# A decoder layer: where one residual is scaled and shifted, where a row of sums of squares is made, and which form its reciprocal root has

## The chip, the cores and the metric

The kernel runs on one core of one Trainium2 chip. The metric is the time of one execution on the device in microseconds (us); the kernel before was run three times. The engines are TensorE (PE, with its weight loads as PEld), VectorE (DVE), ScalarE (ACT), GpSimd (POOL) and the queue engine SyncE (SP), which only issues transfers here. Each engine works through its own list of instructions in order.

## The reference

One layer over 1024 positions of width 1024 with 16 learned meta tokens in front, all in float32:

```python
h = layer_norm(concat([meta, x]), ln_emb_g, ln_emb_b)
proj = h @ w_in                       # q, k, v, xr, gr, 512 columns each
attn = stick_breaking(q, k, v)        # 8 heads of 64
lru = rg_lru(conv(xr), ...) * gelu(gr)
mixed = concat([rms_norm(attn, attn_norm_g), rms_norm(lru, lru_norm_g)]) @ w_out
h = layer_norm(ALPHA * h + mixed, ln1_g, ln1_b)          # ALPHA = 2 ** 0.25
h = layer_norm(ALPHA * h + peer(h), ln2_g, ln2_b)        # retrieval of 16 of 16384 experts per head
return h[:, 16:]
```

Two things in it matter here. The residual `ALPHA * h` of the first layer norm needs that norm's own scale and shift: with the normalised input n it is `n * (ALPHA * g) + ALPHA * b`. And each RMS norm is a factor per position, so it can be put on the product with `w_out` afterwards: 1 / sqrt(mean of squares + 1e-5), one number for each row.

## The kernel before, in words

Positions lie on the 128 partitions, eight tiles of them (j = 0 to 7), the width of 1024 along the free axis. A float32 product is made of three passes of split operands (`mm3`, L126: low x high, high x high, high x low), so each operand is split once: ACT rounds the high part, DVE subtracts it for the low part (`split`, L122; DVE's part is L124).

The stages that matter here, with their times in the profiled execution:

1. **Front** (0 to about 50 us). Nine input tiles `xt` are loaded. DVE makes their statistics, ACT normalises them in place (L281), and POOL issues eight transfers of the normalised tiles to a scratch tensor `xh_d` in device memory (L283). PE transposes the tiles in three groups (L287 to L292), ACT puts scale and shift on the transposed copy (L294), and the copy is split into `hT` (L297, L299, L300). PE begins the projections with it (`pieces`, L223) while later groups are still being made.
2. **Recurrent part** (to about 200 us): `lru_in` (DVE's convolution, `y`, L346 and L348), `lru_gates`, and the values of the attention (`values_w` splits the weights `v`, `values` multiplies). The pools `lr` and `l2` of this stage take the memory that the front's pools `ga` and `lw` give back.
3. **Attention**, four pairs of heads p, each over eight tiles j. `att_a` makes scores, two sigmoids, a running product (DVE scan `om`, L481) and a product (DVE `be`, L482) for each of two heads; `att_b` transposes the result, copies it out of the accumulators (L505, L507) and multiplies it with the values (`po`, L513). While p is 0 to 2, projections for the next pair are put between. At p = 2, j = 6, the projection's memory is given back and the output weights are loaded and split (`load_wo`, L445); also the scale and shift of the first layer norm (`eg`, `eb`), which ACT multiplies by ALPHA (L592, L593). At p = 3 the recurrent half of the out-projection goes between instead: `lru_load` (L552) brings a tile `hr` of `xh_d` back, POOL multiplies it by `eg` and adds `eb` (L556, L557), `lru_mix` (L560) adds the product to it on DVE (L567) and stores it to `ah_d`. `hr` and the raw output weights share one name (`raw`) with two buffers. `att_a` also has POOL copy two small operands (`qz`, L465).
4. **Out-projection** (`mix_out`, about 556 to 645 us). `prep(j)` (L626) loads the attention tile, squares it (`sq`, one buffer), splits it, and makes the sums of squares `ss` by four matmuls with a column of ones (L633) and the reciprocal root `rra` by `rsqrt_small` (L131: ACT root, DVE reciprocal, and one step of improvement in four DVE instructions of which three have two inputs from memory). `body(j)` (L638) runs the 24 matmuls of each tile in two halves of 512 columns, adds each half to the residual (L645) and takes the layer norm, whose own root is `rsqrt_one` (L143: the step of improvement in three DVE instructions, each with one input tensor and numbers per partition). `tail(j)` (L648) transposes and splits the result and has POOL scale and shift it (L651, L652). In program order `prep(j + 1)` stands ahead of `body(j)`.
5. The expert retrieval, to the end.

The order on each engine is not the program order. The library's scheduler plays the program through with estimated durations and issues on each engine, when it is free, the ready instruction that comes first in program order. Instructions that go through `W` or `pin` keep their place behind what stands ahead of them on their engine. Once planned, the order is fixed, and each engine waits at an instruction whose inputs are late.

## Time and profile before

| | |
|---|---|
| median of three runs | 2960.87 us (2960.4 to 2962.03) |
| profiled execution | 2963.82 us, span 2962.0 us |
| busy in the span | PE 2783.2, DVE 2487.0, POOL 1453.4, ACT 1148.1 us |
| mean granted TensorE clock | 0.973 |

The profile is of one execution. A busy share is a mean over stages with different limits, so each stage is read by itself: what its engines do, which of them waits for what, and which steps are on the chain that ends last. The granted clock is a share of full speed: 1.00 is 2.4 GHz and 0.50 is 1.2 GHz. A wait is put down to the instruction that released it.

### The profile page before, as it was taken

The numbers are of one execution on the slowest core, as the hardware profiler recorded it, in microseconds if no ns is written. First come the engines' busy times: TensorE is split into PE (matmuls) and PEld (weight loads), VectorE is DVE, ScalarE is ACT, GpSimd is POOL, SyncE is SP. The second block draws the span as 40 slices with busy tenths as digits, with TensorE's granted clock in tenths as the row PEclk, the third lists the DMA queues.
The fourth block names the chain that finished last, engine by engine and source line by source line (L and its number), as shares of the span: only waits on it lengthen the run. The fifth ranks groups of instructions, "written<-read, shape, count | busy, mean of one in ns | idle before, by whom it ended". The sixth has DMA issues, their size and how long they took to land.

```text
span 2962.0 us, 44399 instructions
## 1 busy us (share of the span) xinstructions
PE 2783.2 (94%) x16311; PEld 2492.6 (84%) x16311; DVE 2487.0 (84%) x4610; ACT 1148.1 (39%) x2245; POOL 1453.4 (49%) x1202
## 2 busy tenths in 40 slices
PE   7999988889879989899989999999999999999997
PEld 6997766679879988889888888888888888888886
DVE  6246667768999999998769999999999999899997
ACT  6445553452212239787752223222222232222222
POOL 0003223343676655645435555556555666665653
PEclk9999988899989999999999999999999999999999
DMA  5123143413656668888789999999999999999992
GB/s 175 30 79 72 39 99 125 149 52 109 218 182 231 229 222 275 276 272 265 236 286 343 353 351 345 347 357 350 335 356 359 349 340 353 350 346 352 334 325 79
DMA packets 353946, 736.32 MB, mean 249 GB/s; under 512 B 26032, under 2 KB 164272, under 8 KB 353728
## 3 DMA queue, kind: packets, MB, share of 16 engines
q0 software_dynamic: 114304, 415.35, 39.5%
q1 hardware_dynamic: 234816, 316.03, 31.7%
q8 instruction: 128, 2.10, 0.3%
q10 hardware_dynamic: 4608, 2.10, 0.2%
q14 instruction: 90, 0.74, 0.1%
HBM read 645.24 MB, written 79.69 MB: 245 GB/s over the span
## 4 chain that ended last, share of the span: by engine, by line
PE 34%; DVE 23%; issue 17%; POOL 12%; DMA 11%; ACT 3%; SPq 0%; POOLq 0%; DVEq 0%; ACTq 0%
POOL row L894 9%; DMA row<-up,idx 6%; DVE row L113 4%; PE pp L127 3%; PE dps L127 3%; PE pp L128 3%; PE dps L129 3%; PE dps L128 3%; PE pp L129 3%; DVE dl L124 2%; DMA row<-down,idx 2%; PE g L1026 2%; PE po L513 2%; DVE h1s L1082 2%; PE z L127 2%
## 5 line engine op out<-in xcount | busy, mean ns | idle before, releaser
L127 PE MATMUL dps<-hTd,dl 128*128 128x320 f32 x2048 | 651.2, 318 | 47.0 <-DVE dl L124 40.7
L129 PE MATMUL dps<-hTd,dh 128*128 128x320 f32 x2048 | 646.6, 316 | 2.0 <-DVE hTd L124 2.0
L128 PE MATMUL dps<-hTd,dh 128*128 128x320 f32 x2048 | 647.3, 316 | 0.0
L894 POOL DMA_INDIRECT row<-down,idx x256 | 357.6, 1397 | 226.5 <-DVE act L113 188.8
L894 POOL DMA_INDIRECT row<-up,idx x256 | 343.6, 1342 | 233.9 <-DVE h1s L1082 196.3
L127 PEld LDWEIGHTS dps<-hTd,dl 128*128 128x128 f32 x2048 | 391.2, 191 | 53.0 <-DVE dl L124 32.9
L127 PE MATMUL ups<-uh,wl 128*128 128x512 f32 x1024 | 406.9, 397 | 2.6 <-DVE wl L124 2.0
L128 PE MATMUL ups<-uh,wh 128*128 128x512 f32 x1024 | 406.9, 397 | 0.0
L129 PE MATMUL ups<-ul,wh 128*128 128x512 f32 x1024 | 406.2, 397 | 0.5 <-DVE ul L124 0.5
L128 PEld LDWEIGHTS dps<-hTd,dh 128*128 128x128 f32 x2048 | 391.5, 191 | 3.0
L129 PEld LDWEIGHTS dps<-hTd,dh 128*128 128x128 f32 x2048 | 390.7, 191 | 2.3 <-DVE hTd L124 2.3
L1082 DVE SCALAR_TENSOR_TENSOR h1s<-row,gws,h1s 128x1024 f32<-128x1024 f32 x256 | 328.2, 1282 | 29.6 <-DMA row<-up,idx 27.5
L113 DVE CUSTOM_DVE_ANT_0 row<-row,h1s 128x1024 f32<-128x1024 f32 x256 | 307.1, 1221 | 36.8 <-DMA row<-down,idx 34.3
L123 ACT ACTIVATE wh<-gl 128x640 fp32r<-128x640 f32 x128 | 101.3, 792 | 606.4 <-DVE gl L1138 344.6
L894 POOL DMA_INDIRECT row<-up,idh x128 | 185.4, 1448 | 233.3 <-DVE acc L1072 84.4
L124 DVE TENSOR_TENSOR dl<-raw,dh 128x1024 fp32r<-128x1024 f32 x144 | 192.5, 1338 | 64.3 <-ACT dh L123 57.7
L129 PEld LDWEIGHTS ups<-ul,wh 128*128 128x128 f32 x1024 | 193.3, 189 | 48.3 <-DVE ul L124 1.0
L127 PEld LDWEIGHTS ups<-uh,wl 128*128 128x128 f32 x1024 | 193.2, 189 | 47.6 <-DVE wl L124 2.4
L128 PEld LDWEIGHTS ups<-uh,wh 128*128 128x128 f32 x1024 | 193.1, 189 | 44.0
L894 POOL DMA_INDIRECT row<-down,idh x128 | 162.2, 1267 | 136.2 <-DVE ach L113 23.8
L123 ACT ACTIVATE uh<-raw 128x1024 fp32r<-128x1024 f32 x128 | 133.0, 1056 | 176.5 <-PE keep L128 167.0
L113 DVE CUSTOM_DVE_ANT_0 row<-row,acc 128x1024 f32<-128x1024 f32 x128 | 176.1, 1381 | 13.0 <-DMA row<-down,idh 13.0
(583 smaller groups left out, 6194.3 us busy)
## 6 DMA issues: line engine op xcount, KB each, us to landing
raw<-downT SPq DMA_DIRECT2D x128, 512.0 KB
raw<-up SPq DMA_DIRECT2D x128, 512.0 KB
Gd<-gst SPq DMA_DIRECT2D x20, 2048.0 KB
gl<-Gd SPq DMA_DIRECT2D x128, 320.0 KB
ge_d<-ge SPq DMA_DIRECT2D x56, 320.0 KB
gex<-ge_d SPq DMA_DIRECT2D x56, 320.0 KB
wraw<-w_in SPq DMA_DIRECT2D x20, 512.0 KB
raw<-wq SPq DMA_DIRECT2D x16, 512.0 KB
```

The lines of the kernel that those rows point to most:

```text
L113: return lambda *a, **k: pin(getattr(V, name)(*a, **k))
L123: A.activation(hi, src, AF.Copy)
L124: V.tensor_tensor(lo, src, hi.bitcast(F32), op=ALU.subtract)
L127: PE.matmul(o, ll, rh, start=start, stop=False, **kw)
L128: PE.matmul(o, lh, rh, start=False, stop=False, **kw)
L129: PE.matmul(o, lh, rl, start=False, stop=stop, **kw)
L513: PE.matmul(po[64 * e:64 * e + 64], vt[:m, b, p * P + 64 * e:p * P + 64 * e + 64], aTs[e][:m, b], start=(b == 0), stop=(b == nb - 1))
L894: G.indirect_dma_start(out=row, out_offset=None, in_=src, in_offset=bass.IndirectOffsetOnAxis(ap=ix, axis=0))
L1026: PE.matmul(gpt[:, q], bt[:, q], at[:, q], start=True, stop=True)
L1082: pin(V.scalar_tensor_tensor(h1s[:, j], row, gws[:, j, s:s + 1], h1s[:, j], op0=ALU.mult, op1=ALU.add))
```

## The change

The scale and shift of the residual move from POOL at p = 3 to DVE at the front: `eg` and `eb` are loaded and multiplied by ALPHA there, in the pool `ga`, and after the three groups DVE multiplies and adds each of the eight tiles `xt` in place; SP instead of POOL then stores them to `xh_d`. At p = 3 the tile from `xh_d` is used as it comes. In `mix_out`, the sums of squares of a tile and their root move from `prep(j)` to `body(j)`, between the two halves of its matmuls; both halves are added to the residual after the second one, and the root has the form of `rsqrt_one`, whose two small tiles it now shares with the layer norm.

```diff
@@ front @@
                 for j in range(j0, j1):
                     n = NM if j == 0 else P
                     A.activation(xts[j][:n], xts[j][:n], AF.Identity, bias=nm9[:n, j:j + 1], scale=rs9[:n, j:j + 1])
-                    if j > 0:
-                        G.dma_start(xh_d[(j - 1) * P:j * P, :], xts[j])
...
                 for xr, gen in convs.values():
                     next(gen)
+            eg = load_vec(ga, 0, "eg")
+            eb = load_vec(ga, 1, "eb")
+            A.activation(eg, eg, AF.Copy, scale=ALPHA)
+            A.activation(eb, eb, AF.Copy, scale=ALPHA)
+            for j in range(1, NT + 1):
+                V.tensor_tensor(xts[j], xts[j], eg, op=ALU.mult)
+                V.tensor_tensor(xts[j], xts[j], eb, op=ALU.add)
+                SY.dma_start(xh_d[(j - 1) * P:j * P, :], xts[j])
@@ lru_load @@
                 SY.dma_start(hr, xh_d[j * P:(j + 1) * P, :])
-                G.tensor_tensor(hr, hr, eg, op=ALU.mult)
-                G.tensor_tensor(hr, hr, eb, op=ALU.add)
@@ attention, p == 2 and j == 6 @@
-                        eg = load_vec(mp, 0, "eg")
-                        eb = load_vec(mp, 1, "eb")
-                        A.activation(eg, eg, AF.Copy, scale=ALPHA)
-                        A.activation(eb, eb, AF.Copy, scale=ALPHA)
@@ mix_out @@
             def prep(j):
                 mh, ml, sq = first if j == 0 else mixed(0, j)
                 SY.dma_start(h1[j], ah_d[j * P:(j + 1) * P, :])
-                mv = wm.tile([P, 1], F32, name="mva")
-                rra = wm.tile([P, 1], F32, name="rra")
-                ss = sps.tile([P, 1], F32, name="ss")
-                for c in range(4):
-                    PE.matmul(ss, sq[:, c], ones, start=(c == 0), stop=(c == 3))
-                V.tensor_scalar(mv, ss, 1.0 / AW, EPS, op0=ALU.mult, op1=ALU.add)
-                rsqrt_small(rra, mv, P, 1, "ra", wm)
-                return mh, ml, rra
-
-            def body(j, mh, ml, rra):
+                return mh, ml, sq
+
+            def body(j, mh, ml, sq):
+                halves = []
                 for hf in range(2):
...
                         mm3(ps, mh[:, c], ml[:, c], wh[:, cs], wl[:, cs], c == 0, c == 3)
+                    halves.append((cs, ps))
+                    if hf == 0:
+                        mv = wm.tile([P, 1], F32, name="mva")
+                        rra = wm.tile([P, 1], F32, name="rra")
+                        ss = sps.tile([P, 1], F32, name="ss")
+                        for c in range(4):
+                            PE.matmul(ss, sq[:, c], ones, start=(c == 0), stop=(c == 3))
+                        V.tensor_scalar(mv, ss, 1.0 / AW, EPS, op0=ALU.mult, op1=ALU.add)
+                        rsqrt_one(rra, mv, P)
+                for cs, ps in halves:
                     V.scalar_tensor_tensor(h1[j][:, cs], ps, rra, h1[j][:, cs], op0=ALU.mult, op1=ALU.add)
```

## Rows read from the trace of the kernel before

**Rows 1.** The table of stretches: busy time of each engine in each, the granted clock of TensorE, the share of the transfer engines that was busy, and the GB/s that they moved.

```profile
403.00:420.00 17.00, 8.58 (x64) 5.85 (x62) 9.73 (x8) 10.84 (x23) 2.89 (x9) 0.84 1.09 251
...
435.00:556.00 121.00, 99.33 (x529) 73.11 (x527) 86.62 (x65) 41.32 (x109) 51.47 (x39) 0.87 0.33 113
556.00:645.00 89.00, 77.56 (x411) 65.19 (x412) 65.27 (x158) 52.38 (x109) 30.97 (x12) 0.92 0.31 105
```

**Rows 2.** DVE in order of time at the end of the front and after it: start, duration, what, and in brackets the idle time before it and who ended it.

```profile
31.54 0.36 DVE L297 CAST hT<-tm 128x384 fp32r<-128x384 f32 x1 [5.17 <-ACT tm L294]
...
43.08 0.36 DVE L297 CAST hT<-tm 128x384 fp32r<-128x384 f32 x1 [4.13 <-ACT tm L294]
...
54.34 1.19 DVE L124 TENSOR_TENSOR v<-wraw,v 128x1024 fp32r<-128x1024 f32 x1
...
86.93 1.23 DVE L124 TENSOR_TENSOR v<-wraw,v 128x1024 fp32r<-128x1024 f32 x1 [16.45 <-ACT v L123]
```

**Rows 3.** DVE by line and shape, 160 to 200 us: an instruction with two inputs of 128x1024 from memory (count, busy us, mean ns, idle before it).

```profile
L416 DVE TENSOR_TENSOR y<-t,gg 128x1024 f32<-128x1024 f32 x4 | 4.9, 1224 | 21.8 <-ACT gg L414 21.8
```

**Rows 4.** PE's waits by who released them, 20 to 160 us: total, times, longest.

```profile
PE pp L129 <- DVE v L124: 0.8, 1, 0.8
```

**Rows 5.** PE in order of time at the start of the values: start, duration, what. The matmuls overlap; the starts give their pace.

```profile
55.81 0.28 PE L127 MATMUL pp<-v,hT 128*128 128x256 f32 x1
55.93 0.28 PE L128 MATMUL pp<-v,hT 128*128 128x256 f32 x1
```

**Rows 6.** SP in order of time where the output weights are first loaded: the transfers as they are issued.

```profile
402.34 0.34 SPq L119 DMA_DIRECT2D eg<-vecs  x1
...
403.26 0.85 SPq L447 DMA_DIRECT2D raw<-w_out  x2
```

**Rows 7.** ACT in order of time there: the second of its two multiplications by ALPHA.

```profile
409.28 1.06 ACT L593 ACTIVATE eb<-eb 128x1024 f32<-128x1024 f32 x1 [0.28 <-DMA eb<-vecs]
```

**Rows 8.** The chain that ended last, 395 to 560 us, in order of time: start, duration, what.

```profile
460.32 3.05 DVE om L481
...
471.67 2.34 POOL raw L557
474.07 1.15 POOL qz L465
...
539.07 4.42 DVE om L481
```

**Rows 9.** The same view a little earlier, 380 to 436 us: the transfer of the first output weights.

```profile
403.68 13.94 DMA raw<-w_out
```

**Rows 10.** PE in order of time: its longest idle time there, in brackets.

```profile
419.54 0.65 PE L473 MATMUL z<-KS,QS 128*128 128x344 f32 x1 [8.12 <-ACT om L478]
```

**Rows 11.** POOL by line and shape, 430 to 556 us.

```profile
L556 POOL TENSOR_TENSOR raw<-raw,eg 128x1024 f32<-128x1024 f32 x8 | 23.3, 2907 | 10.6 <-issue 8.6 <-DMA raw<-xh_d 1.8
L557 POOL TENSOR_TENSOR raw<-raw,eb 128x1024 f32<-128x1024 f32 x8 | 22.3, 2782 | 0.5
```

**Rows 12.** DVE by line, 287 to 354 us: the sixteen scans and products of pair p = 1, in which POOL has no product or sum of its own.

```profile
L481 DVE TENSOR_TENSOR_SCAN om<-om 128x144 f32<-128x144 f32 (+7 forms) x16 | 22.1, 1386 | 4.1 <-ACT om L478 4.1
L482 DVE TENSOR_TENSOR be<-be,om 128x144 f32<-128x144 f32 (+7 forms) x16 | 12.4, 777 | 1.3
```

**Rows 13.** The same, 432.7 to 546 us: the sixteen scans and products of pair p = 3, which have the same shapes, and the low parts of its tiles.

```profile
L481 DVE TENSOR_TENSOR_SCAN om<-om 128x144 f32<-128x144 f32 (+7 forms) x16 | 30.2, 1892 | 3.5 <-ACT om L478 3.5
L482 DVE TENSOR_TENSOR be<-be,om 128x144 f32<-128x144 f32 (+7 forms) x16 | 27.6, 1730 | 0.8
L124 DVE TENSOR_TENSOR ml<-ml,mh 128x512 fp32r<-128x512 f32 x9 | 12.2, 1355 | 2.1 <-ACT mh L123 2.1
```

**Rows 14.** PE's waits, 430 to 556 us.

```profile
PE po L513 <- DVE aT L505: 18.5, 6, 5.1
```

**Rows 15.** DVE by line in the out-projection, 556 to 645 us: the root of the sums of squares, one instruction of the layer norm's root, the low parts, and ten of the sixteen sums with the residual.

```profile
L141 DVE TENSOR_TENSOR rra<-rra,rat 128x1 f32<-128x1 f32 x8 | 8.0, 1001 | 0.1
L645 DVE SCALAR_TENSOR_TENSOR acc<-z,rra,acc 128x512 f32<-128x512 f32 x10 | 7.4, 743 | 4.9 <-PE z L129 4.9
...
L124 DVE TENSOR_TENSOR ml<-ml,mh 128x512 fp32r<-128x512 f32 x7 | 4.8, 684 | 0.2 <-ACT mh L123 0.2
L138 DVE TENSOR_TENSOR rat<-rra 128x1 f32<-128x1 f32 x8 | 4.3, 533 | 0.0
L139 DVE TENSOR_TENSOR rat<-rat,mva 128x1 f32<-128x1 f32 x8 | 4.2, 530 | 0.1
...
L148 DVE TENSOR_SCALAR lnrt<-lnrs,lnve 128x1 f32<-128x1 f32 x8 | 2.2, 272 | 0.3
...
L140 DVE TENSOR_SCALAR rat<-rat 128x1 f32<-128x1 f32 x8 | 1.2, 148 | 0.1
```

**Rows 16.** DVE in order of time at one place of it.

```profile
584.01 2.37 DVE L139 TENSOR_TENSOR rat<-rat,mva 128x1 f32<-128x1 f32 x1
```

**Rows 17.** POOL in order of time at the same place.

```profile
582.88 3.49 POOL L651 TENSOR_TENSOR acc<-acc,eg 128x1024 f32<-128x1024 f32 x1 [4.79 <-ACT dh L123]
586.45 2.34 POOL L652 TENSOR_TENSOR acc<-acc,eb 128x1024 f32<-128x1024 f32 x1
```

**Rows 18.** PE's waits in the out-projection, 556 to 660 us.

```profile
PE ss L633 <- ACT sq L548: 7.9, 4, 3.8
```

**Rows 19.** The chain that ended last, 555 to 690 us: one matmul of a half of 512 columns.

```profile
563.29 0.23 PE z L129
```

## The prediction

> **What bounds the kernel now.** I read four views, in this order: the table of stretches, DVE and POOL by line, the chain that ended last, and the waits of PE.
>
> In the stretches [rows 1] the reader is to see that pair p = 3 takes 121 us in which PE is busy for 99.3, at a granted clock of 0.87, and DVE for 86.6; that POOL has its heaviest load of the early stages just there, 51.5 us; and that the out-projection takes 89 us with PE busy for 77.6. No engine fills either stage; a chain through several of them does.
>
> By line, POOL's 51.5 us are nearly all the sixteen products and sums of the residual, 23.3 + 22.3 = 45.6 us [rows 11]. Beside them DVE becomes slow: the same sixteen scans cost 22.1 us in pair 1 and 30.2 in pair 3, the same sixteen products 12.4 and 27.6 [rows 12, 13]. The low parts take 1.355 us in pair 3 and 0.684 in the out-projection [rows 13, 15]. The excess is 8.1 + 15.2 + 9 x 0.671 = 29.3 us. All of these have two inputs from memory, and they stop while POOL runs such an instruction: a 128x1 product lasted from 584.01 to 586.38, and POOL's product from 582.88 to 586.37 [rows 16, 17].
>
> The chain shows whether that matters. It goes through the held scans, one of 4.42 us, and through POOL itself, where a copy `qz` stands behind a sum (2.34 + 1.15 us) [rows 8]. PE waits 18.5 us for DVE's copies in this stage [rows 14].
>
> **The change part by part.**
>
> *Front, DVE.* Added: 16 instructions of 128x1024 with two inputs. Such a one takes 1.224 us [rows 3], so 19.6 us on DVE. A tile is ready for them when its group is transposed. DVE has idle spans of 5.17 and 4.13 us behind the first two groups [rows 2], which hold the four instructions of two tiles and three more. The other nine, 11.0 us, come when the third group is done. In program order they stand ahead of the values' weights, so I put them in front of the second low part of `v`, which ended at 55.5 us. They also stand ahead of the first convolution; that one's memory (`y0`, `y1`) now lies where `eg` and `eb` lie, and it must wait for them in any case. Behind all this DVE has 16.45 us idle before 86.93 [rows 2], so only PE's wait for `v` counts. PE waits 0.8 us for it now [rows 4]. Without the low part PE can run two of three passes of its two accumulators, 32 matmuls at 0.12 us [rows 5], 3.8 us. 11.0 less 3.8 leaves 7.2; some of the nine will slip into short gaps of the third group, so I take +5 us. The ends: 0, if the planner finds room for all of it, and +12, if PE can do nothing meanwhile and `eg` and `eb` cost ACT another 1 us (one multiplication is 1.06 [rows 7]). A gain has no source there: nothing in the front waits for POOL's eight issues.
>
> *Front, SP.* The eight stores now wait in SP's list for DVE's sums, and the later loads of `w_in` stand behind them. Those feed low parts that start at 86.93 us or later; the same 16.45 us of idle time cover it, and I cost it at nothing, inside the +12 if not.
>
> *Before pair 3.* Removed: two loads of 512 KB that SP issues just ahead of the output weights [rows 6], and two multiplications on ACT. The first weights are 13.94 us on the chain [rows 9]; ACT waits for them in order, with the next scores' sigmoids behind, and PE stands idle for 8.12 us [rows 10]. In that stretch 251 GB/s move at full load [rows 1], so 1.05 MB less are 4.2 us. I take -4; the ends are 0, if the other transfers of the stretch set the landing, and -6.3 with the two multiplications of 1.06 us.
>
> *Pair 3.* Removed: 45.6 us on POOL, and with them the 29.3 us of held DVE time and POOL's 3.5 us ahead of `qz`. Added: nothing; `hr` comes ready. What is late next is PE. 121 less 99.3 leaves 21.7 us of idle PE, and more can go only if the clock rises above 0.87. I take -18, close to PE's 18.5 us of waiting for DVE's copies. The ends: -3.5, if only the place with `qz` goes and matmuls take every other one, and -29.
>
> *Out-projection, the root.* The three instructions with two inputs cost 8.0 + 4.3 + 4.2 = 16.5 us in eight tiles, where an unheld one is 0.148, so 24 x 0.148 = 3.6 and the excess 12.9 [rows 15]. `rsqrt_one` has numbers per partition in their place, 0.272 us for the dearest while POOL does the same work, and one instruction fewer. But POOL's own 31.0 us stay [rows 1], and the low parts (two inputs) come next on DVE and will take part of the hold. I count half, -6.5.
>
> The Trainium skill ("SBUF — State Buffer", section "Who interferes with whom") lists `tensor_scalar` among the instructions that can take the port pair that DVE and GpSimd share, which would speak against this edit. By that the new root would be held like the old one, this part would be 0 and the sum some 6 us smaller. The 128x1 instructions measured beside POOL contradict it for this shape (0.148 and 0.272 us, eight each [rows 15]), so I go by the rows; the sum that it gives, -17, would lie inside the forecast's span, with a chance of 0.03 out of the forecast's.
>
> *Out-projection, the place of the sums.* PE waits 7.9 us at `ss` for the square of the next tile [rows 18]; moved, it uses a square made long before, and the load that was waited for is needed a tile later anyway. Against that, the first half is added only after the root, so up to one addition of 0.743 us per tile comes later [rows 15], and there is one buffer `sq`: the next square waits for `ss` in the middle of a tile, and the next low part, which overwrites the square's source, waits for that. I let gain and loss cancel but for +0.5, so the stage gives -6. The ends: -15 (12.9, and a little of PE's wait) and +5 (additions late in most of the tiles and no hold saved).
>
> **Sum.** +5 - 4 - 18 - 6 = -23 us. The profiled execution took 2963.82 us; 2963.82 - 23 = 2940.8. It is 2.95 us above the median of the runs shown, 2960.87, so against that 2938.
>
> **The rivals.**
>
> *All of it comes out.* PE's clock rises once its pauses are short, and pair 3 gives 27, the out-projection 12, the weights 5, the front costs 2: -42, 2919 us. For it: the clock of 0.87, and that the chain runs through the holds. Against: PE's 99.3 busy us. Chance 0.16.
>
> *PE takes the chain over.* The matmuls of `lru_mix` stand in PE's list between the attention's, and the stage keeps its length but for 7 us; weights -3, out-projection -4, front +7: -7, 2954 us. For it: PE busy 82% of the stage. Against: 18.5 us of waiting for DVE. Chance 0.13.
>
> *Hidden anyway.* The holds go, but DVE and ACT then wait where PE's order was planned, and the front eats the rest: within 6 us, 2961. Chance 0.08.
>
> *Slower, through the one buffer `sq`.* Place: between two tiles of the out-projection. After `ss` come the square (as an estimate as long as a low part, 0.7), and the low part of 0.684, which has two inputs and may meet a pair of POOL's, 3.49 + 2.34 us [rows 17]. The second half of the matmuls covers 12 x 0.23 = 2.8 us [rows 19]. At worst 0.7 + 0.7 + 5.8 - 2.8 = 4.4 us idle in each of seven gaps, 31 us. The stage then costs +31 instead of giving 6, and the sum is +14: 2975 us. It decides from 17 / 7 = 2.4 us per gap on, where it eats the other three terms. For it: POOL is busy for a third of the stage. Against: today's low parts of these tiles are unheld, 0.684 us. Chance 0.07.
>
> **How the numbers follow.** The forecast's own case has 0.56 and spans -14 to -32. What a measurement of this kernel can tell from no change is about 0.2%, 6 us. Faster by more: 0.56 + 0.16 + 0.13 = 0.85. Within: 0.08. Slower: 0.07. The sum of all favourable ends is -50 and of all others +13.5. The range 2916 to 2957 leaves out the two last cases and a tail of the first rival, together 0.2.
>
> **What would show it.** Pair 3: scans and products back at 22 and 12 us, low parts at 0.68, the stage near 103 us, POOL under 10. If the scans are back and the stage is still above 112, PE had it. Before pair 3: PE's idle time near 4 us in place of 8.12. Front: PE idle for some 5 us between 50 and 66 us, released by DVE's `v`; if it is 0, the planner found room. Out-projection: the three instructions of the root below 0.3 us each, held low parts in their place, the stage at 83 us; a longer stage with PE waiting for `ml` is the one buffer. The prediction is wrong as a whole if pair 3 does not shorten by 10 us.

## The result and the profile after

The changed kernel takes 2930.98 us (median of 6 runs, 2926.4 to 2932.32); the kernel before took 2961.45 in the same session. The ratio is 0.9894, with a 95% interval of 0.9877 to 0.9911: faster by 1.1%. The prediction was 2938 with a range of 2916 to 2957. The profiled execution took 2931.09 us with a span of 2929.3, so it stands at the median.

To see where the 32.7 us between the two spans come from, I cut both traces at five instructions that both kernels have: the first copy of an attention output (`ao`, on ACT), the copies of the tiles (p = 2, j = 5) and (2, 6), the last copy (3, 7), and the first copy of the retrieval's scores (`sb`). All times are starts in ACT's order of time, in us.

| stretch | before | after | difference | predicted |
|---|---|---|---|---|
| start to the first `ao` (front, recurrent part) | 236.5 | 250.9 | +14.4 | +5 |
| first `ao` to that of (2, 5) | 174.35 | 174.33 | 0.0 | 0 |
| to that of (2, 6): the output weights | 22.2 | 18.2 | -4.0 | -4 |
| to the last `ao`: pair 3 | 125.1 | 93.6 | -31.5 | -18 |
| to the first `sb`: out-projection | 109.6 | 101.5 | -8.1 | -6 |
| to the end: retrieval | 2294.3 | 2290.7 | -3.6 | 0 |

So the total is right, but two of its terms are off by 9 and 13 us in opposite directions; that they nearly cancel is luck. The last row is no effect of the change that I can show: with the same code there, one execution each of this kernel and of the twelve below lies between 2285.5 and 2296.9.

First the table of stretches of the kernel after (columns as in [rows 1]).

```profile
60.00:80.00 20.00, 11.14 (x54) 9.19 (x55) 17.90 (x27) 6.61 (x10) 0.55 (x4) 0.64 0.42 139
...
445.00:535.00 90.00, 87.18 (x533) 64.31 (x531) 57.42 (x66) 41.39 (x110) 6.04 (x24) 1.00 0.41 138
535.00:616.00 81.00, 74.68 (x412) 63.53 (x412) 62.81 (x149) 50.88 (x107) 30.84 (x12) 0.96 0.33 112
```

Pair 3 is now a stretch of 90 us that PE fills (87.2 us at a granted clock of 1.00); before, it was 121 us with 99.3 at 0.87 [rows 1]. POOL went from 51.5 to 6.0 us there. In the front, PE is busy for only 11 of the 20 us from 60 to 80, and the granted clock is 0.64 in the mean; from 58.4 to 72 us it is 0.50, the level of 1.2 GHz.

**The front.** DVE in order of time:

```profile
32.08 0.36 DVE L295 CAST hT<-tm 128x384 fp32r<-128x384 f32 x1 [5.55 <-ACT tm L292]
...
38.20 1.22 DVE L306 TENSOR_TENSOR xt<-xt,eg 128x1024 f32<-128x1024 f32 x1 [0.50 <-ACT eg L303]
...
60.14 2.35 DVE L307 TENSOR_TENSOR xt<-xt,eb 128x1024 f32<-128x1024 f32 x2
62.41 1.56 DVE L352 TENSOR_SCALAR y<-xr,ch 128x1040 f32<-128x1040 f32 x2
63.88 1.30 DVE L354 SCALAR_TENSOR_TENSOR y<-xr,ch,y 128x1040 f32<-128x1040 f32 x1
65.17 1.22 DVE L124 TENSOR_TENSOR v<-wraw,v 128x1024 fp32r<-128x1024 f32 x1
66.30 1.30 DVE L354 SCALAR_TENSOR_TENSOR y<-xr,ch,y 128x1040 f32<-128x1040 f32 x1
67.60 1.20 DVE L124 TENSOR_TENSOR v<-wraw,v 128x1024 fp32r<-128x1024 f32 x1
```

The gap behind the first group is as empty as before (5.55 us; 5.17 in [rows 2]). The first product starts at 38.20 and had waited for ACT, which scales `eg` only at 37.09. The last sum ends at 62.5, then the first two convolutions (`y`) come, and between their instructions the low parts of `v`. The second of them ends at 68.8; before, at 55.5 [rows 2]. That is 13.3 us later. PE's waits from 20 to 160 us, and PE's first matmuls with `v`:

```profile
PE pp L129 <- DVE v L124: 9.3, 1, 9.3
PE pp L127 <- ACT v L123: 4.3, 1, 4.3
```

```profile
58.38 0.58 PE L127 MATMUL pp<-v,hT 128*128 128x256 f32 x1 [4.29 <-ACT v L123]
58.76 0.42 PE L128 MATMUL pp<-v,hT 128*128 128x256 f32 x1
58.97 0.41 PE L127 MATMUL pp<-v,hT 128*128 128x256 f32 x1
59.19 0.41 PE L128 MATMUL pp<-v,hT 128*128 128x256 f32 x1
68.86 0.58 PE L129 MATMUL pp<-v,hT 128*128 128x256 f32 x1 [9.25 <-DVE v L124]
```

PE runs four matmuls, then the fifth (L129) needs the low part and waits 9.25 us. Together 13.6 us of waiting, where there were 0.8 for the low part [rows 4] and 0.4 for the high one. The clock adds to it: the sixteen matmuls between 58.4 and 72 us take 4.35 us at 0.50, so at 1.00 they would take some 2 us less, as an estimate.

**Pair 3.** DVE by line, 440 to 531 us, the same sixteen scans and products as in [rows 13], and PE's waits from 440 to 535:

```profile
L487 DVE TENSOR_TENSOR_SCAN om<-om 128x144 f32<-128x144 f32 (+7 forms) x16 | 22.1, 1384 | 3.8 <-ACT om L484 3.8
L488 DVE TENSOR_TENSOR be<-be,om 128x144 f32<-128x144 f32 (+7 forms) x16 | 12.3, 772 | 1.1
L124 DVE TENSOR_TENSOR ml<-ml,mh 128x512 fp32r<-128x512 f32 x9 | 6.1, 682 | 2.3 <-ACT mh L123 2.3
```

```profile
PE po L519 <- DVE aT L511: 1.8, 3, 1.0
```

The scans are back at 22.1 us (30.2 before), the products at 12.3 (27.6), the low parts at 0.68 (1.36): 29.5 us fewer on DVE. PE's wait for DVE's copies is 1.8 us in place of 18.5 [rows 14].

**The output weights.** SP in order of time, and PE's longest idle time there:

```profile
416.90 0.82 SPq L453 DMA_DIRECT2D raw<-w_out  x2
...
418.80 1.01 SPq L119 DMA_DIRECT2D eg<-vecs  x1
419.86 0.83 SPq L119 DMA_DIRECT2D eb<-vecs  x1
```

```profile
432.97 0.46 PE L479 MATMUL z<-KS,QS 128*128 128x144 f32 x1 [2.37 <-DMA QS<-ql]
```

Two loads of a vector are there again, now behind the first two weights: they are `g1` and `b1` of the layer norm in the out-projection. Their memory has the tags `eg` and `eb`, and since nobody holds it any more, the scheduler issues them at 418.8 in place of 538.0. PE's longest idle time there, 8.12 us [rows 10], became 2.37, and what ends it is another transfer (`QS`).

**The out-projection.** DVE by line, 536 to 620 us, and PE's waits from 536 to 632:

```profile
L124 DVE TENSOR_TENSOR hTd<-tm,hTd 128x512 fp32r<-128x512 f32 x10 | 11.1, 1113 | 0.1
...
L124 DVE TENSOR_TENSOR ml<-ml,mh 128x512 fp32r<-128x512 f32 x7 | 9.1, 1301 | 0.5 <-ACT sq L554 0.5
...
L149 DVE TENSOR_SCALAR lnrt<-lnrt 128x1 f32<-128x1 f32 x16 | 2.4, 152 | 0.4
...
L148 DVE TENSOR_SCALAR lnrt<-rra,mva 128x1 f32<-128x1 f32 x8 | 2.2, 271 | 0.2
...
L150 DVE TENSOR_SCALAR rra<-rra,lnrt 128x1 f32<-128x1 f32 x8 | 1.7, 212 | 0.2
```

```profile
PE z L127 <- DVE ml L124: 3.3, 3, 2.1
```

The root is never held: 0.271, 0.152 and 0.212 us, although POOL is busy for the same 31 us. The low parts `ml` are held now, 1.30 us each where they had 0.68 [rows 15], and PE waits 3.3 us for them (whether they are what the root gave up, the experiments tell). PE's 7.9 us at `ss` [rows 18] are gone.

### The profile page after: what moved, and what is told of

It reads as the page before. It is cut to its first block, busy times and chain, and to the rows that moved or that the text cites. A ratio compares the mean times of both kernels' runs of the same rounds, so it can differ in the third digit from the quotient of the medians.

```text
span 2929.3 us, 44388 instructions
## 1 busy us (share of the span) xinstructions
PE 2772.4 (95%) x16311; PEld 2487.8 (85%) x16311; DVE 2474.4 (84%) x4618; ACT 1150.2 (39%) x2245; POOL 1401.4 (48%) x1178
## 4 chain that ended last, share of the span: by engine, by line
PE 45%; DVE 15%; issue 7%; POOL 6%; DMA 4%; ACT 2%; POOLq 0%; SPq 0%; DVEq 0%; ACTq 0%
PE ups L127 6%; PE dps L127 6%; PE ups L128 6%; PE ups L129 6%; PE dps L129 6%; PE dps L128 6%; POOL row L898 4%; DVE row L113 3%; PE g L1030 2%; DVE dl L124 2%; DMA row<-up,idx 2%; PE keep L129 1%; PE keep L128 1%; PE keep L127 1%; PE z L127 1%
## 5 line engine op out<-in xcount | busy, mean ns | idle before, releaser
L129 PE MATMUL dps<-hTd,dh 128*128 128x320 f32 x2048 | 647.2, 316 | 0.0
L129 PE MATMUL ups<-ul,wh 128*128 128x512 f32 x1024 | 406.3, 397 | 0.5 <-DVE ul L124 0.5
L129 PEld LDWEIGHTS dps<-hTd,dh 128*128 128x128 f32 x2048 | 391.0, 191 | 0.1
L123 ACT ACTIVATE wh<-gl 128x640 fp32r<-128x640 f32 x128 | 101.1, 791 | 530.0 <-DVE gl L1142 315.5
L129 PEld LDWEIGHTS ups<-ul,wh 128*128 128x128 f32 x1024 | 193.1, 189 | 48.3 <-DVE ul L124 1.0
```

Of the source, the lines that this page charges most:

```text
L123: A.activation(hi, src, AF.Copy)
L129: PE.matmul(o, lh, rl, start=False, stop=stop, **kw)
```

## The experiments

Twelve kernels were run. The table has, for each, the stretches of the table above (one profiled execution each) and the ratio of its runs to those of the kernel before, which took 2961 to 2966 us in these sessions.

| kernel | first `ao` | weights | pair 3 | out-proj. | rest | median | ratio, interval |
|---|---|---|---|---|---|---|---|
| changed kernel | 250.9 | 18.2 | 93.6 | 101.5 | 2290.7 | 2931.0 | 0.9894, 0.9877 to 0.9911 |
| values first | 235.4 | 16.8 | 94.0 | 100.7 | 2293.5 | 2916.6 | 0.9852, 0.9829 to 0.9875 |
| no scaling on ACT | 245.9 | 15.9 | 93.8 | 100.9 | 2290.1 | 2927.2 | 0.9889, 0.9869 to 0.9909 |
| no front products | 236.4 | 17.9 | 93.7 | 101.1 | 2285.7 | 2913.3 | 0.9838, 0.9817 to 0.9859 |
| both | 233.9 | 16.5 | 94.1 | 101.0 | 2293.3 | 2914.3 | 0.9832, 0.9813 to 0.9851 |
| mix as before | 248.6 | 17.5 | 95.8 | 109.0 | 2296.9 | 2944.6 | 0.9945, 0.9933 to 0.9958 |
| place only | 249.8 | 17.7 | 93.8 | 110.6 | 2293.5 | 2940.0 | 0.9922, 0.9909 to 0.9936 |
| root only | 249.4 | 17.7 | 93.6 | 102.3 | 2285.5 | 2933.6 | 0.9904, 0.9892 to 0.9917 |
| POOL load, two inputs | 250.1 | 18.2 | 108.5 | 99.2 | 2294.5 | 2947.6 | 0.9945, 0.9928 to 0.9961 |
| POOL load, one input | 251.2 | 15.9 | 99.8 | 101.4 | 2296.2 | 2940.2 | 0.9914, 0.9887 to 0.9942 |
| loads back | 250.5 | 21.6 | 93.4 | 97.4 | 2293.0 | 2932.9 | 0.9897, 0.9875 to 0.9919 |
| late vectors | 249.5 | 14.9 | 93.4 | 101.1 | 2292.9 | 2930.4 | 0.9890, 0.9867 to 0.9914 |
| best | 234.8 | 15.5 | 93.7 | 101.5 | 2296.0 | 2913.1 | 0.9818, 0.9800 to 0.9836 |

Read a column downwards: where an edit doesn't reach, the stretches agree within 1 to 4 us (the out-projection lies between 97.4 and 101.5 with the same code there), and that is the scatter that one execution has; the rest scatters by 11. A stretch therefore tells more of an edit than the time does.

**Values first.** The tiles of `values_w` get a pool of their own, opened before the front, and the first half's weights are split ahead of the residual.

```diff
+        vp = vx.enter_context(tc.tile_pool(name="vp", bufs=1, reuse_waits="tile"))
...
+            v0 = values_w(0)
             eg = load_vec(ga, 0, "eg")
...
-                v0 = values_w(0)
                 lru_in(1)
```

> The values' weights are split ahead of the residual's sixteen instructions in program order; their tiles get a pool of their own, nothing else differs from the changed kernel (median 2931.0 us, 14.4 us late at the first product with the values of the attention). Theory: the 14.4 us are PE waiting for the low part of the values' weights behind the sixteen on DVE; then PE's two waits of 4.3 and 9.3 us for v nearly go and the time falls by 10 to 14 us, to 2917 to 2921. Rival: they come from the loads and stores of the front, which share the transfer engines with the weights; then the waits move to another releaser and the time stays within 3 us of 2931.

Measured: 2916.6 us, and the first `ao` at 235.4, 15.5 us earlier. DVE and PE in order of time:

```profile
38.05 1.23 DVE L124 TENSOR_TENSOR v<-wraw,v 128x1024 fp32r<-128x1024 f32 x1 [0.50 <-ACT v L123]
39.98 1.23 DVE L124 TENSOR_TENSOR v<-wraw,v 128x1024 fp32r<-128x1024 f32 x1
```

```profile
55.33 0.38 PE L127 MATMUL pp<-v,hT 128*128 128x256 f32 x1 [1.35 <-ACT xr L241]
```

The low parts of `v` are ready at 41.2, the sixteen instructions run to 66.9 behind them, and the front costs nothing: all sixteen fit where DVE has nothing urgent. The cost was the order, not the work. The tiles of `v` also lie elsewhere in memory here; that this is not the cause I take from the changed kernel, where ACT writes the first high part of `v` at 54.80, while the residual's sums still run, and DVE comes to the low parts without idle time.

**No scaling on ACT.** DVE's product and sum take ALPHA along as a constant, and ACT's two multiplications go.

```diff
-            A.activation(eg, eg, AF.Copy, scale=ALPHA)
-            A.activation(eb, eb, AF.Copy, scale=ALPHA)
...
-                V.tensor_tensor(xts[j], xts[j], eg, op=ALU.mult)
-                V.tensor_tensor(xts[j], xts[j], eb, op=ALU.add)
+                V.scalar_tensor_tensor(xts[j], xts[j], ALPHA, eg, op0=ALU.mult, op1=ALU.mult)
+                V.scalar_tensor_tensor(xts[j], eb, ALPHA, xts[j], op0=ALU.mult, op1=ALU.add)
```

> ALPHA goes into the DVE instructions (three-operand form), so that the scale and shift need nothing of ACT. Theory: DVE's gap of 5.55 us behind the first group stays empty in the changed kernel only because ACT multiplies the scale at about 37 us; now four instructions fall into it and PE's wait for v shortens by 4 to 5 us: 2926 to 2927. Rival: the planner does not see the gap, or the tiles are not free then; the gap stays, and the time is 2931 or 1 us more for the longer instructions.

Measured: first `ao` 5.0 us earlier; the time 2927.2, an interval that overlaps that of the changed kernel. PE's waits and DVE in order of time:

```profile
PE pp L129 <- DVE v L124: 4.5, 1, 4.5
PE pp L127 <- ACT v L123: 4.3, 1, 4.3
```

```profile
25.63 1.22 DVE L304 SCALAR_TENSOR_TENSOR xt<-xt,eg 128x1024 f32<-128x1024 f32 x1
```

Now the gap behind the first group is used, from 25.63 on, and PE's wait for the low part falls from 9.3 to 4.5. The front still costs 9.4 us against the kernel before: filling the gap, as the prediction had it, is worth only the smaller part.

**No front products.** The sixteen instructions, the two multiplications by ALPHA and the two loads of `eg` and `eb` are left out, so the residual lacks the scale, the shift and ALPHA; the eight stores stay on SP, where they now wait for nothing of DVE.

```diff
-            eg = load_vec(ga, 0, "eg")
-            eb = load_vec(ga, 1, "eb")
-            A.activation(eg, eg, AF.Copy, scale=ALPHA)
-            A.activation(eb, eb, AF.Copy, scale=ALPHA)
             for j in range(1, NT + 1):
-                V.tensor_tensor(xts[j], xts[j], eg, op=ALU.mult)
-                V.tensor_tensor(xts[j], xts[j], eb, op=ALU.add)
                 SY.dma_start(xh_d[(j - 1) * P:j * P, :], xts[j])
```

> The residual's products, sums and its scale and shift are left out (the residual of the first layer norm is then the bare normalised tile), the eight stores stay on SP. Theory of the DVE queue: the whole 14.4 us at the front go, 2916 to 2918. Rival of the transfers: the stores stay and only two loads go, so at most 4 us go, 2927 or more.

Measured: first `ao` at 236.4, as in the kernel before, and PE's wait for `v` is 0.8 us again. So the stores on SP cost nothing by themselves, and what this run leaves out costs all 14.4. That it is the place of DVE's sixteen, and not the two loads, only values first tells, which keeps both and still has the first `ao` at 235.4.

**Both** of the first two edits together.

> The first two edits together. Theory: as the values are no longer behind the sixteen, the second edit has little left to give: 2915 to 2920, within 3 us of the first edit alone, and some 12 us below the changed kernel. Rival: both work through the length of DVE's queue and add up, 4 to 5 us below the first alone.

Measured: first `ao` at 233.9, 1.5 us ahead of values first alone; the time 2914.3.

**The out-projection in parts.** Three kernels: *mix as before* undoes the whole edit of the stage; *place only* keeps the sums between the halves, with the old root; *root only* keeps the new root, with the sums ahead of each tile.

```diff
# place only
-                        rsqrt_one(rra, mv, P)
+                        rsqrt_small(rra, mv, P, 1, "ra", wm)
# root only, in prep(j)
+                for c in range(4):
+                    PE.matmul(ss, sq[:, c], ones, start=(c == 0), stop=(c == 3))
+                V.tensor_scalar(mv, ss, 1.0 / AW, EPS, op0=ALU.mult, op1=ALU.add)
+                rsqrt_one(rra, mv, P)
```

> The changed kernel with the out-projection of the kernel before: sums of squares and the six-instruction root ahead of each tile. It prices the whole edit of that stage. Theory A: the stage's 8.1 us (107.9 less 99.8) come from the edit, so the time goes back by about 8, to 2939 us, and the low parts of the stage come down from 1.30 to about 0.7 us while the root's 128x1 products are held again at 1 us or more. Rival B: POOL's 31 us of products and sums decide the stage whichever of DVE's instructions meets them, and the 8 us came from how the stage is entered: then this run is within 2 us of 2931.

> The changed kernel with the sums between the halves as they are, but with the six-instruction root. Theory A, as the prediction split it: the root is the larger part, so about 6 us of the edit are lost here, 2937 us, and the root's three products are held again for 12 us of DVE in all. Rival C: the place is the larger part, because PE no longer waits for the square (7.9 us of waiting at the sums before): then this run stays within 3 us of 2931, held root or not.

> The changed kernel with the new root, but with the sums ahead of each tile as before. Theory A: the root is the larger part, so nearly all of the gain stays, 2932 us, and PE waits for the square again for some 8 us without a cost. Rival C: the place is the larger part, 2936 to 2938 us, with PE's wait for the square back on the path.

Measured: the stage takes 109.0, 110.6 and 102.3 us, against 101.5 with both edits. So the new root gives 109.0 - 102.3 = 6.7 with the old place and 110.6 - 101.5 = 9.1 with the new one; the new place costs 1.6 with the old root and gives 0.8 with the new one, which is within the scatter. By the medians the order is the same: the loss of the root is 9.0 us, that of the place 2.7, of both 13.6; in that last one 6 us lie in the rest of the kernel and not in the stage, and I can't say whether they belong to the edit. DVE by line, 536 to 640 us, first in *mix as before*:

```profile
L124 DVE TENSOR_TENSOR hTd<-tm,hTd 128x512 fp32r<-128x512 f32 x10 | 9.0, 902 | 0.4 <-ACT hTd L123 0.4
...
L124 DVE TENSOR_TENSOR ml<-ml,mh 128x512 fp32r<-128x512 f32 x7 | 4.8, 684 | 0.2 <-ACT mh L123 0.2
```

then in *place only*:

```profile
L124 DVE TENSOR_TENSOR ml<-ml,mh 128x512 fp32r<-128x512 f32 x7 | 9.1, 1295 | 0.5 <-ACT sq L554 0.5
...
L138 DVE TENSOR_TENSOR rat<-rra 128x1 f32<-128x1 f32 x8 | 5.3, 665 | 0.1
L141 DVE TENSOR_TENSOR rra<-rra,rat 128x1 f32<-128x1 f32 x8 | 5.2, 654 | 0.1
```

and in *root only*, with PE's waits of the same stretch:

```profile
L124 DVE TENSOR_TENSOR hTd<-tm,hTd 128x512 fp32r<-128x512 f32 x10 | 14.2, 1416 | 0.5 <-ACT hTd L123 0.5
...
L124 DVE TENSOR_TENSOR ml<-ml,mh 128x512 fp32r<-128x512 f32 x7 | 6.3, 907 | 0.0
```

```profile
PE ss L633 <- ACT sq L554: 3.9, 3, 3.4
```

The holds move in every version; what differs is whom they meet. The low parts of the stage (`hTd`, `ml` and `hTs`) take 22.4 us together in mix as before, 27.2 in place only, 30.1 in root only and 30.5 in the changed kernel. Which of them is held is not fixed by the code: the new root alone puts most on `hTd` (0.90 to 1.42 us), `ml` has 1.30 us in place only, with the old root, and over the ten kernels with the changed kernel's stage it lies between 0.87 and 1.30 without the stage's length following it (100.7 us at 0.95, 101.5 at 1.30). My reading of the stage's length, which no run isolates, is this: a held low part of `hTd` (1.42 us in root only) belongs to the tail of the tile before, and the stage is as short with it. A held root stands ahead of the additions of its own tile, and the stage is longer. PE's 7.9 us at `ss` were no gain to be had: place only takes them away (0.8 us left), and the stage is no shorter.

**A load on POOL in pair 3.** Sixteen products of 128x1024 on POOL into a tile that nobody reads; the residual comes ready as in the changed kernel. In the second version each is an operation with one input and two constants.

```diff
                 SY.dma_start(hr, xh_d[j * P:(j + 1) * P, :])
+                for _ in range(2):
+                    G.tensor_tensor(dmy, rep, rep, op=ALU.mult)
# one input
+                    G.tensor_scalar(dmy, rep, 1.0, 0.0, op0=ALU.mult, op1=ALU.add)
```

> The changed kernel, and on GpSimd beside each tile of pair 3 two 128x1024 products of two inputs from memory into a tile that nobody reads. The data path is untouched: the residual still comes ready, with no wait for these. Theory A: the stage shortened because GpSimd no longer holds DVE's two-input instructions; then they are held again (sixteen scans near 30 us and their products near 27 in place of 22 and 13), the pair takes 15 to 32 us more, and the time is 2946 to 2963 us. Rival D: it shortened because the residual comes ready and no copy stands behind it on GpSimd: then DVE is held but the time stays within 5 us of 2931.

> As the run with GpSimd's products that nobody reads, but each of them is an operation with one input from memory and two constants, of the same 128x1024. That run took 2947.6 us and held the first six scans of pair 3 (4.0, 4.4 for two, 2.2, 2.4 us). Theory A: GpSimd holds DVE by its second input, so here the scans are unheld (2.40, 0.80 for two, 0.72, 0.72), and the time is within 3 us of 2931. Rival E: any busy GpSimd holds DVE's two-input instructions; then the same scans are held for as long as these operations run, and the time is between 2936 and 2948.

Measured: pair 3 takes 108.5 us with two inputs (+14.9) and 99.8 with one (+6.2). The data path is the same, so POOL's work alone makes this stage longer. The scheduler didn't spread it: as nothing holds it back, it ran almost in one block, from 422 to some 468 us with two inputs and from 424 to 457 with one. DVE in order of time, first with two inputs, then with one; the unheld scans of these three places take 2.40, 0.80 (two of them) and 0.72 us in the changed kernel:

```profile
432.80 4.02 DVE L487 TENSOR_TENSOR_SCAN om<-om 128x1040 f32<-128x1040 f32 x1
446.14 4.39 DVE L487 TENSOR_TENSOR_SCAN om<-om 128x144 f32<-128x144 f32 x2
...
456.61 0.31 DVE L488 TENSOR_TENSOR be<-be,om 128x144 f32<-128x144 f32 x1 [5.83 <-POOL om L485]
459.34 2.21 DVE L487 TENSOR_TENSOR_SCAN om<-om 128x272 f32<-128x272 f32 x1
```

```profile
443.26 1.68 DVE L487 TENSOR_TENSOR_SCAN om<-om 128x144 f32<-128x144 f32 x2
...
449.84 0.31 DVE L488 TENSOR_TENSOR be<-be,om 128x144 f32<-128x144 f32 x1 [3.65 <-POOL om L485]
451.72 1.35 DVE L487 TENSOR_TENSOR_SCAN om<-om 128x272 f32<-128x272 f32 x1
```

DVE by line with two inputs, 440 to 547 us:

```profile
L487 DVE TENSOR_TENSOR_SCAN om<-om 128x144 f32<-128x144 f32 (+7 forms) x16 | 28.8, 1808 | 3.8 <-ACT om L484 3.8
L488 DVE TENSOR_TENSOR be<-be,om 128x144 f32<-128x144 f32 (+7 forms) x16 | 13.8, 864 | 9.2 <-POOL om L485 8.3
...
L458 DVE SCALAR_TENSOR_TENSOR wol<-raw,ch,woh 128x1024 fp32r<-128x1024 f32 x6 | 10.6, 1773 | 2.6 <-ACT woh L457 2.6
```

Most scans beside the block are held, and once it is over they have their length. But a second thing is in it: DVE's product waits for a memset of one column (`om`, L485) that stands behind the block on POOL, 8.3 us in all with two inputs and 5.3 with one. With two inputs the holds are 28.8 - 22.1 = 6.7 us on scans, 13.8 - 12.3 = 1.5 on products, 7.7 - 6.1 = 1.6 on low parts and 10.6 - 7.6 = 3.0 on the low parts of the output weights (`wol`), 12.8 in all. So the run shows that POOL's load is enough to lengthen the stage, and that holds are part of it; it doesn't give the price of the holds alone, since the wait for the small instructions queued on POOL comes on top. Nor is it the load of the kernel before: twelve of the sixteen fall into the stage, 25.0 us of POOL where there were 45.6 [rows 11]. The queue is the test's own: in the kernel before, no wait of PE or DVE from 435 to 556 us is put down to POOL, though the chain passes through it once [rows 8]. Expectation and measurement of the second version differ: I had held the second input of POOL's instruction for the cause, and one input holds too (0.84 us for a scan of 0.40, 1.35 for one of 0.72). The holding is mutual: POOL's own one-input operation takes 1.04 us alone and up to 2.93 beside a scan.

```profile
433.38 2.93 POOL L563 TENSOR_SCALAR dmy<-ident 128x1024 f32<-128x1024 f32 x1
...
453.58 1.04 POOL L563 TENSOR_SCALAR dmy<-ident 128x1024 f32<-128x1024 f32 x1
```

The Trainium skill ("SBUF — State Buffer", section "Who interferes with whom") says that an instruction of DVE with two inputs from SBUF contends with one of GpSimd that reads SBUF, and not with one that only writes it; it sets no second input of GpSimd's as a condition. By that the second version had to hold too, and the trace agrees (0.84 us for a scan of 0.40).

**The loads before pair 3.** *Loads back* puts two loads of 512 KB and ACT's two multiplications back ahead of the output weights, for nobody; *late vectors* keeps the memory of `g1` and `b1` taken until the seventh tile, so that their loads leave this stretch. In *loads back* they leave it too, so these two kernels differ in the four instructions ahead of the weights.

```diff
# loads back; late vectors has an empty tile and a memset of one column in their place
+                        for i, n in enumerate(("eg", "eb")):
+                            dmy.append(load_vec(mp, i, n))
+                            A.activation(dmy[i], dmy[i], AF.Copy, scale=ALPHA)
# both, in lru_load(j)
+                if j == 6:
+                    for t in dmy:
+                        G.tensor_tensor(t[:, :1], t[:, :1], hr[:, :1], op=ALU.mult)
```

> The changed kernel with the two loads of 512 KB and ACT's two multiplications put back ahead of the output weights of pair 3, used by nobody; one element of each is read by GpSimd at the seventh tile of the pair, so that the loads of the second norm's vectors come as late as in the kernel before. Theory A: these four instructions were the 4.0 us by which the step from pair 2 to pair 3 became shorter (22.2 to 18.2), so the step goes back to about 22 and the time to 2935 us. Rival B: the step is shorter because the residual's first load no longer stands where it stood, or because of the holds; then it stays near 18 and the time within 1.5 us of 2931.

> The changed kernel, but the memory of the second norm's two vectors is kept taken until the seventh tile of pair 3, so that their loads (1.05 MB, in the changed kernel issued between the two halves of the first output weights) no longer fall into the step from pair 2 to pair 3. Theory A, transfers set the step: it becomes 3 to 4 us shorter than 18.2, and the time is 2927 us. Rival B: the loads stand behind the weights that ACT waits for, or ACT's two multiplications were what counted; then the step stays at 18 and the time within 1.5 us of 2931.

Measured: the step takes 21.6 us with the loads back and 14.9 with the vectors late, against 18.2; both as theory A had it. Between the two, the four instructions ahead of the weights cost 21.6 - 14.9 = 6.7 us; the changed kernel keeps 21.6 - 18.2 = 3.4 of that, as `g1` and `b1` come into the stretch. PE's waits with the loads back, 410 to 446 us:

```profile
PE z L479 <- ACT om L484: 7.6, 3, 7.2
```

That is the idle time of [rows 10] again, 7.2 us in place of 8.12. The times follow less: 2932.9 (+1.9) and 2930.4 (-0.6), both within their uncertainty. With the loads back the out-projection is 4.1 us shorter than in the changed kernel, which takes the loss back; why, I have not tried. Its `ml` are held less (0.87 us in the mean), but so they are in kernels without such a gain. And the step is 15.9 us in two kernels whose edit lies elsewhere or takes only one of the loads away (no scaling on ACT; POOL load, one input), so of the 3.3 us of late vectors perhaps one to two are its own.

**Best.** Both edits of the front, and the vectors late.

> The version that the runs so far point to: the values' weights ahead of the residual and the residual without a multiplication on ACT (that run took 2914.3 us), and the second norm's vectors loaded late (that alone made the step from pair 2 to pair 3 3.3 us shorter: 14.9 in place of 18.2). If the gains add, the first output of the attention is at 234 us, the step takes 15 us and the time is 2911 us. Rival: what the step gains is waited for later, as the time of the run with the late vectors alone (2930.35) suggests; then the step is 15 us and the time still 2914.

Measured: 2913.1 us, a ratio of 0.9818. First `ao` at 234.8, step 15.5; the step is 1.0 shorter than in *both* (16.5), and the two times can't be told apart. By the medians each is some 17 us faster than the changed kernel and some 50 faster than the one before.

## Why the prediction was right, and where it was not

**Front, DVE: +5 predicted, +14.4 measured, beyond the end of +12.** Here the prediction failed, in two sentences. The first: DVE's idle spans "hold the four instructions of two tiles and three more". The first span was idle, but the instructions weren't ready: the scale came from ACT, which worked through its list of transposed copies first and multiplied `eg` only at 37.09, when that span was over. Four ran where the second span had been (38.20 to 44.04) and three more among the splits of the third group, whose last one ends at 53.4 in place of 49.8; with them the first high part of `v` became late (54.80 in place of 48.79). The second: "Without the low part PE can run two of three passes of its two accumulators, 32 matmuls". The three passes alternate in PE's list, and four matmuls stand ahead of the first one that needs the low part. The trace before could have told: there, too, four run from 53.91 on, and then PE waits the 0.8 us of [rows 4]. The count of nine behind the third group was nearly right (eight start behind its last split, nine after 50 us), though not for its reason. That SP's stores cost nothing was right: the next loads of `w_in` are issued at 66.45 in place of 51.12, but no wait of PE up to 160 us is put down to their weights. Two costs the prediction did not have. Of the first two convolutions, which come free at the same moment, four instructions stand ahead of the second low part, where there were two. And after PE's waits the clock is at 0.50, some 2 us. Values first shows that the whole 14.4 is order.

**Weights: -4 predicted, -4.0 measured**, and loads back returns 3.4 of it. That the number is met is luck: the reason holds only by half. I had reckoned 1.05 MB less in the stretch, but the same amount came back in the form of `g1` and `b1`, behind the first weights in SP's list. What was taken away is worth 6.7 us (loads back against late vectors), about the end of -6.3, and what came in costs 3.3 (late vectors against the changed kernel), each with a scatter of some 2; the prediction had only the first, and too small.

**Pair 3: -18 predicted, -31.5 measured; the end was -29.** The mechanism fits, the size was too small: held time on DVE fell by 29.5 us, PE's wait for its copies from 18.5 to 1.8, and POOL's load put back in part returned 14.9 of the 31.5; no run returns the whole. The prediction capped the gain by PE's 21.7 us of idle time and said that more can go only if the clock rises above 0.87. It rose to 1.00: PE's busy time for the same matmuls fell from 99.3 to 87.2, and its idle time from 21.7 to 2.8; 12.1 + 18.9 = 31. The rows before had the first number too: 99.3 x 0.87 = 86.4. I had put this into a rival with a chance of 0.16. The rows that spoke for it stood there: a clock of 0.87 [rows 1] in a stage in which PE stands still for up to 5.1 us at a time [rows 14].

**Out-projection: -6 predicted (-6.5 root, +0.5 place), -8.1 measured.** The parts are 6.7 to 9.1 for the root, and for the place between a loss of 1.6 and a gain of 0.8. Of the 12.9 us of held root [rows 15] some 50 to 70% came out, where I had counted half; the rest sits on the low parts, as said, which take 30.1 us together with the root alone where they took 22.4. That `ml` alone went from 0.68 to 1.30 us is not what the root gave up: with the old root in the new place it has 1.30 too. The 0.148 us for an unheld product came from an instruction with one input, but fits: in place only the product L139, with two, takes 0.154 where it is not held. The sentence that the place cancels was right, and so was the bound from 128x1 instructions with numbers per partition: they are not held. The rows show this shape alone, so the prediction's word "contradict" was too strong.

**The rivals.** "PE takes the chain over" is half true: PE fills pair 3 now, but only after all the excess had gone. "Hidden anyway" is refuted by pair 3, which became 31.5 us shorter. "Slower, through the one buffer" had its place right and its price wrong: PE waits 3.3 us in all for `ml`, not 17 or more. "All of it comes out" was right for pair 3, near for the weights and too high for the out-projection; behind the first `ao` the kernel gained 47.1 us, and the front took 14.4 back.

## What to carry to other kernels

When work moves to an engine that has idle time, check what stands behind it in that engine's list and whether its inputs exist at the time of the gap: here the same sixteen instructions cost 14 us ahead of the values' weights and nothing behind them. When stalls of PE go, count the clock too: in a stage below full clock the busy time of the same matmuls falls with the stalls, and PE's old busy time is no floor. When one instruction is taken out of a hold by another engine, the hold can land on others with two inputs, as it did on `hTd` with the new root alone, so ask who waits for those. And an instruction that is taken away frees its memory: look what the scheduler moves into the gap before counting the gap as gained.

## What the runs showed of the hardware

- A one-input operation of POOL holds DVE's scans too (0.84 us for one of 0.40, 1.35 for one of 0.72), and is held by them: 1.04 us alone, up to 2.93. Beside POOL's product of two inputs such scans took 2.2 us each.
- After PE had stood for 4.3 us, and soon for 9.25 more, the granted clock was 0.50 (1.2 GHz) from 58.4 to 72 us; PE worked without a wait from 68.86 on, and from 76 us the clock was 1.00 (2.4 GHz); the matmuls of 256 columns start 0.21 us apart at the lower level (58.76 to 59.19), where they had 0.12 [rows 5]. With the values first, where PE does not stand there, the granted clock from 60 to 80 us is 1.00.
- Freed memory moves transfers: two loads went forward by some 120 us because their tag had lost its user, into the very stretch that two other loads had left.
